# Weight sums of seven block products: from VectorE additions to accumulating transfers on GpSimd's queue, with tiles moved by 32 bytes

## The chip, the cores and the metric

The kernel runs on one core of one Trainium2 chip, in one launch. The metric is the time of one execution in microseconds (us); the time before is a median of 449.09 us over 3 runs (448.83 to 450.26). The weights stand in the chip's main memory (HBM) and are brought into SBUF, the on-chip memory that the engines read. Each engine works through its instructions in order: PE (TensorE, matrix products), ACT (ScalarE), DVE (VectorE), POOL (GpSimd) and SP (SyncE, which only issues transfers here). A transfer can be issued by SP or by POOL; the engine that issues it goes on, and the sixteen DMA engines of the core carry it out.

## The reference

One layer on 256 tokens of width 1024, everything in f32:

```
h = rms_norm(x, mix_norm_gain)
proj = h @ w_in                      # 1024 x 6144
xa, ga, qm, km, vm, qx, g_logits = split(proj)
y_a = rg_lru(conv(xa)) * gelu(ga)    # recurrent branch, width 512
y_b = block attention(qm, km, vm)    # width 512
y_c = cross attention(qx, mem)       # width 512
gates = sigmoid(g_logits).reshape(256, 3, 1024)
merged = sum over n of gates[n] * (y_n @ w_branch[n])
x = x + merged @ w_out
h = rms_norm(x, ffn_norm_gain)
x = x + (gelu(conv(h @ w_ffn_gate)) * (h @ w_ffn_up)) @ w_ffn_down
return rms_norm(x, final_norm_gain)
```

The change touches one piece of `proj`: the 1024 columns of `g_logits` that belong to gate 0 (`h` with a 1024 x 1024 part of `w_in`).

## The kernel before

**Weights as units.** All weight matrices are packed ahead of the launch into one array `ws` of units of 128 x 2048 f32 (1 MB). A unit is loaded by SP into a tile `wraw` (three buffers, L143). ACT rounds it to the high part `whi` (L189), and DVE subtracts that from the unit to get the low part `wlo` (L190); in the text, this pair is called the split of a unit. TensorE then makes each product as three matmuls: high x high, high x low, low x high. `ahead()` runs after each unit is consumed: it issues loads up to 4 steps ahead and splits up to 2 steps ahead. Two sequences made by `unit_plan()` set this: `PLAN` (which unit is which piece of a weight) and `STEPS` (in which order units are split and used). A scheduler of the framework then places each instruction on its engine's list by the order in which the program writes it and by what each needs; tiles come from pools with a fixed number of buffers, so a load or a split also waits until its buffer is free.

**Gate 0 by seven products.** The weight of gate 0 is cut into 2 x 2 blocks of one unit each, B11, B12 (the second 512 columns), B21 and B22 (the second half of the contraction). The 256 tokens are cut into two halves, so that the activations too form 2 x 2 blocks. Gate 0 needs seven block products (`product()`, L779) in place of eight: with B11, B21 and B22 themselves, and with four sums, T1 = B11 + B12, T3 = B12 + B22, T2 = T1 + B22 and T4 = T2 + B21. The activations' sums S1 to S4 are in the tiles `sh` and `sl`. The products stand between other units in the order of `STEPS`: B11, branch(1,0), T2, branch(2,0), T1, a half of gate(1,1), T3, its other half, B21, branch(1,1), B22, a half of gate(2,1), T4. `branch(n, half)` multiplies the output of branch n with half of its projection; its matmuls are at L247 to L249, those of `product()` at L785.

**How the sums are made before.** `block_t1()` runs when B11 has been split: SP loads B12 as two tiles of 128 x 1024 (`b12`, L160), and two DVE additions (`add2()`, L155) add it to B11's own tile `wraw`, which becomes T1. `block_t2()` runs when T2 is to be split: SP loads B22 into `b22` (L166), two additions make T3 in place of B12, and two write T2 into two tiles `t2`. When T4 is due, two additions add B21 to `t2`. Each sum is then split like a unit, in two halves of 128 x 1024.

**What the names in the profile are.** The program's names lose their digits there: `b12` and `b22` read `b`, the tiles `t2` read `t`, `p1` reads `p`, `u2` reads `u`. `ybh`, `ych` and `ycl` are the high and low parts of the outputs of branch 1 and 2, `mg` the sum of the gated branches, `gt` a gate, `fgb` the broadcast final gain, which POOL loads by a transfer of its own much later (L904). `PAD` is the width of an unused tile at the start of the first pool; every tile of the pools behind it lies that much further in each partition of SBUF.

Of the kernel before, what the change touches and what calls it, by code (L numbers as in the profile page):

```python
# [11 lines left out]
OP = mybir.AluOpType  # L12
# [84 lines left out]


LAG = 2
PAD = 232  # L100
WARM = 8
PLAN, STEPS = unit_plan()
NU = len(PLAN) - 2
# [4 lines left out]
def hybrid_trunk(ctx: ExitStack, tc: tile.TileContext, ws, xw, xv, xn, mt, mn, pp, lw, fg, out):  # L108
    nc = tc.nc
    V, A, T, G = nc.vector, nc.scalar, nc.tensor, nc.gpsimd  # L110

    cst = ctx.enter_context(tc.tile_pool(name="cst", bufs=1))
    cst.tile([128, PAD], F32, name="pad")
    wp = ctx.enter_context(tc.tile_pool(name="wp", bufs=3))
# [19 lines left out]
    raw, hi, lo = {}, {}, {}  # L134
# [12 lines left out]
    blk = {}  # L147
    HW = UW // 2

    def halves(t):  # L150
        return [t[:, :HW], t[:, HW:]]

    def add2(o, a, b):
        for x, y, z in zip(o, a, b):
            V.tensor_add(x, y, z)  # L155

    def block_t1(b11):
        blk["B12"] = [s4("b12", sh=(128, HW)) for _ in range(2)]
        for t, c in zip(blk["B12"], (0, HW)):
            nc.sync.dma_start(t, ws[NU - 2, :, c:c + HW])  # L160
        blk["T1"] = halves(raw[b11])
        add2(blk["T1"], blk["T1"], blk["B12"])

    def block_t2():
        b22 = ip.tile([128, UW], F32, name="b22", tag="sc", bufs=1)
        nc.sync.dma_start(b22, ws[NU - 1])  # L166
        blk["B22"] = halves(b22)
        blk["T3"] = blk["B12"]
        add2(blk["T3"], blk["B12"], blk["B22"])
        blk["T2"] = [s4("t2", sh=(128, HW)) for _ in range(2)]  # L170
        add2(blk["T2"], blk["T1"], blk["B22"])

    def split_next(parts=1):
        i = st["spl"]
        u = STEPS[i]
        h = wp.tile([128, UW], F32R, name="whi")
        l = wp.tile([128, UW], F32R, name="wlo")
        if u == "T2":
            block_t2()
        elif u == "T4":  # L180
            blk["T4"] = blk["T2"]
            add2(blk["T4"], blk["T2"], halves(raw[i0["B21"]]))
        if isinstance(u, str):
            src = list(zip(blk[u], halves(h), halves(l)))
        else:
            w = UW // parts
            src = [[t[:, p * w:(p + 1) * w] for t in (raw[u], h, l)] for p in range(parts)]
        for r, hh, ll in src:
            A.copy(hh, r)  # L189
            V.tensor_sub(ll, r, hh.bitcast(F32))  # L190
        hi[i], lo[i] = h, l
        if u == i0["B11"]:
            block_t1(u)
        st["spl"] += 1

    T2S = STEPS.index("T2")
    i0 = {"B11": STEPS[T2S - 2], "B21": STEPS[STEPS.index("B22") - 2]}
# [7 lines left out]
    def ahead():  # L205
        u = st["u"] - 1
        n = max(x for x in STEPS[:min(u + LA_D, NS - 1) + 1] if not isinstance(x, str))
        while st["dma"] <= n:
            dma_next()
        while st["spl"] <= min(u + LA_S, NS - 1):  # L210
            split_next()
# [75 lines left out]
    for k in range(KC):  # L287
        t = ip.tile([128, 1024], F32, name="xw", tag="s4", bufs=15)
# [24 lines left out]
    def s4(nm, dt=F32, sh=(128, 4, S)):  # L313
        t = ip.tile(list(sh), dt, name=nm, tag="s4", bufs=15)
        return t
# [17 lines left out]
    for k in range(KC):  # L333
# [14 lines left out]
        for j, (a, b) in enumerate(((h, xh), (h, xl), (l, xh))):  # L348
            for m in range(4):
                c = slice(512 * (k % 4) + m * 128, 512 * (k % 4) + m * 128 + 128)  # L350
                T.matmul(b0[m][:, :S], lhsT=a[:, c], rhs=b[:, k, :], start=(k == 0 and j == 0),  # L351
                         stop=(k == KC - 1 and j == 2))
    st["spl"] = st["u"] = 2
    split_next(2)
    split_next(2)
    ahead()
    sq = s4("sq", sh=(128, D))
# [47 lines left out]
    e, z, y, q, n8 = [cst.tile([128, 4], F32, name=f"sp{i}") for i in range(5)]  # L405
# [308 lines left out]
    sh, sl = a8p.tile([128, 4, 4, 128], F32R, name="sh", tag="a8"), a8p.tile([128, 4, 4, 128], F32R, name="sl", tag="a8")  # L714
# [135 lines left out]
    for i in range(2):  # L850
        t = a8p.tile([128, 4, 2, S], F32R, name="h2", tag="a8")
# [73 lines left out]
    def ffn_gate(f, bk):  # L925
        g = gp[f % 3]
        t = fp.tile([128, 2, S], F32, name="tcv", bufs=3)
        t2 = join(bk)
        V.tensor_mul(g[:, :, 2:], t2, rb2x)
        for m in range(2):  # L930
            b = 2 * f + m
            A.activation(t[:, m, :], g[:, m, 2:], AF.Identity, scale=par("fw", 48 + b), bias=par("fb", b))
            V.scalar_tensor_tensor(t[:, m, :], g[:, m, 1:1 + S], par("fw", 24 + b), t[:, m, :], op0=OP.mult, op1=OP.add)
            V.scalar_tensor_tensor(t[:, m, :], g[:, m, 0:S], par("fw", b), t[:, m, :], op0=OP.mult, op1=OP.add)  # L934
        A.activation(t, t, AF.Gelu_apprx_tanh)  # L935
        return t
# [45 lines left out]
    for f in range(1, 13):  # L982
        if f < 12:
# [4 lines left out]
            t = ffn_gate(f, gbk)  # L988
# [14 lines left out]
    for i, (t, c0, c1) in enumerate(FIN):  # L1003
        o = dz[i - 3][:, :256] if i > 2 else db[t][c0 // 512][:, c0 % 512:c0 % 512 + c1 - c0]
        V.scalar_tensor_tensor(yf[:, t, c0:c1], o, rs2[:, t:t + 1], (yf if i > 2 else x2)[:, t, c0:c1], op0=OP.mult,
                               op1=OP.add)
        x = slice(t, t + 1)
# [98 lines left out]
```

## Time and profile before

| | before |
|---|---|
| median of 3 runs | 449.09 us (448.83 to 450.26) |
| profiled execution, whole | 449.81 us |
| its span, first to last instruction | 448.0 us |
| mean granted TensorE clock | 0.994 of full speed |
| PE busy | 438.4 us, 98% of the span |
| DVE busy | 345.5 us, 77% |
| ACT busy | 274.9 us, 61% |
| POOL busy | 18.9 us, 4% |
| moved by transfers | 84.38 MB, mean 188 GB/s |

The span is shorter than the execution by what lies around it, 1.8 us here, and the profiled execution is 0.72 us above the median of the runs. Busy shares are means over the whole span. To find where an engine that is busy 98% of the time still loses some, one looks at shares in short stretches, at the waits of that engine, and then at the list of instructions around a wait. The granted clock is given as a share of 2.4 GHz: 1.00 is that level, 0.50 is 1.2 GHz.

### The profile page before, as it was taken

The numbers are of one execution on the slowest core, as the hardware profiler recorded it, in microseconds if no ns is written. First come the engines' busy times: TensorE is split into PE (matmuls) and PEld (weight loads), VectorE is DVE, ScalarE is ACT, GpSimd is POOL, SyncE is SP. The second block draws the span as 40 slices with busy tenths as digits, with TensorE's granted clock in tenths as the row PEclk, the third lists the DMA queues.
The fourth block names the chain that finished last, engine by engine and source line by source line (L and its number), as shares of the span: only waits on it lengthen the run. The fifth ranks groups of instructions, "written<-read, shape, count | busy, mean of one in ns | idle before, by whom it ended". The sixth has DMA issues, their size and how long they took to land.

```text
span 448.0 us, 6270 instructions
## 1 busy us (share of the span) xinstructions
PE 438.4 (98%) x2486; PEld 383.2 (86%) x2486; DVE 345.5 (77%) x458; ACT 274.9 (61%) x374; POOL 18.9 (4%) x21
## 2 busy tenths in 40 slices
PE   9999999999999899999999999999999999999994
PEld 9999879998888688888888888888888888888883
DVE  6679799999699997848767798766676677677664
ACT  6675989986655547554347676554554554554543
POOL 2000200130000000000001200000000000000011
PEclk9999999999999899999999999999999999999999
DMA  8975753556525356265445555545545555545102
GB/s 300 412 283 189 282 197 140 189 191 223 191 93 189 98 192 274 94 228 201 168 169 199 199 203 189 189 181 190 195 178 200 196 178 208 193 162 222 53 0 94
DMA packets 13852, 84.38 MB, mean 188 GB/s; under 512 B 1792, under 2 KB 2304, under 8 KB 4608
## 3 DMA queue, kind: packets, MB, share of 16 engines
q1 hardware_dynamic: 13392, 82.95, 50.3%
q0 software_dynamic: 144, 0.52, 0.5%
q10 hardware_dynamic: 288, 0.52, 0.3%
q8 instruction: 19, 0.31, 0.3%
q14 instruction: 9, 0.07, 0.0%
HBM read 82.94 MB, written 1.05 MB: 187 GB/s over the span
## 4 chain that ended last, share of the span: by engine, by line
PE 91%; DVE 6%; ACT 1%; issue 1%; DVEq 0%; ACTq 0%
PE mm L234 18%; PE mm L237 9%; PE ac L976 5%; PE ac L977 5%; PE ac L978 5%; PE ac L247 4%; PE ac L248 4%; PE ac L249 4%; PE mm L785 4%; PE mm L247 3%; PE mm L248 3%; PE mm L249 3%; PE mm L219 3%; PE mm L220 3%; PE mm L221 3%; PE mm L351 3%
## 5 line engine op out<-in xcount | busy, mean ns | idle before, releaser
L190 DVE TENSOR_TENSOR wlo<-wraw,whi 128x2048 fp32r<-128x2048 f32 (+1 forms) x74 | 164.1, 2220 | 68.8 <-ACT whi L189 68.5
L189 ACT CAST whi<-wraw 128x2048 fp32r<-128x2048 f32 (+1 forms) x74 | 135.9, 1839 | 79.4 <-PE mm L234 29.8
L234 PE MATMUL mm<-h,whi 128*128 128x512 f32 x352 | 88.8, 392 | 0.0
L234 PEld LDWEIGHTS mm<-h,whi 128*128 128x128 f32 x352 | 63.7, 189 | 11.6
L237 PEld LDWEIGHTS mm<-h,wlo 128*128 128x128 f32 x352 | 48.6, 190 | 3.8
L237 PE MATMUL mm<-h,wlo 128*128 128x256 f32 x352 | 49.7, 282 | 0.0
L976 PE MATMUL ac<-whi,ah 128*128 128x512 f32 x92 | 35.9, 392 | 0.0
L977 PE MATMUL ac<-wlo,ah 128*128 128x512 f32 x92 | 35.8, 391 | 0.0
L978 PE MATMUL ac<-whi,al 128*128 128x512 f32 x92 | 35.7, 390 | 0.0
L921 ACT COPY join<-mm 128x256 f32<-128x256 f32 x44 | 15.9, 364 | 18.6 <-PE mm L237 18.5
L935 ACT ACTIVATE tcv<-tcv 128x512 f32<-128x512 f32 x12 | 7.6, 632 | 27.0 <-DVE tcv L934 27.0
L219 PE MATMUL mm<-xh,whi 128*128 128x256 f32 x80 | 22.8, 284 | 0.0
L220 PE MATMUL mm<-xl,whi 128*128 128x256 f32 x80 | 22.6, 283 | 0.0
L221 PE MATMUL mm<-xh,wlo 128*128 128x256 f32 x80 | 22.6, 283 | 0.0
L978 PEld LDWEIGHTS ac<-whi,al 128*128 128x128 f32 x92 | 17.3, 188 | 3.8 <-DVE al L945 0.2
L976 PEld LDWEIGHTS ac<-whi,ah 128*128 128x128 f32 x92 | 17.3, 188 | 3.5 <-ACT ah L944 0.3
L977 PEld LDWEIGHTS ac<-wlo,ah 128*128 128x128 f32 x92 | 17.3, 188 | 3.2
L247 PE MATMUL mm<-whi,xh 128*128 128x512 f32 x48 | 18.9, 395 | 0.0
L249 PE MATMUL mm<-whi,xl 128*128 128x512 f32 x48 | 18.8, 392 | 0.0
L248 PE MATMUL mm<-wlo,xh 128*128 128x512 f32 x48 | 18.7, 391 | 0.0
L922 DVE TENSOR_TENSOR join<-mm,join 128x256 f32<-128x256 f32 x44 | 17.4, 417 | 0.3 <-ACT join L921 0.3
L219 PEld LDWEIGHTS mm<-xh,whi 128*128 128x128 f32 x80 | 15.4, 192 | 0.3 <-issue 0.3
(332 smaller groups left out, 914.5 us busy)
## 6 DMA issues: line engine op xcount, KB each, us to landing
wraw<-in_ws_dram SPq DMA_DIRECT2D x68, 1024.0 KB, 4.8
xw<-in_xv_dram SPq DMA_DIRECT2D x6, 388.0 KB, 6.4
wraw<-in_ws_dram SPq DMA_DIRECT2D x4, 512.0 KB, 9.9
x<-in_xn_dram SPq DMA_DIRECT2D x1, 1024.0 KB, 13.8
mnat<-in_mn_dram SPq DMA_DIRECT2D x1, 1024.0 KB, 5.5
mr<-in_mt_dram SPq DMA_DIRECT2D x1, 1024.0 KB, 4.8
b<-in_ws_dram SPq DMA_DIRECT2D x2, 512.0 KB, 6.8
b<-in_ws_dram SPq DMA_DIRECT2D x1, 1024.0 KB, 4.7
```

The lines of the kernel that those rows point to most:

```text
L189: A.copy(hh, r)
L190: V.tensor_sub(ll, r, hh.bitcast(F32))
L219: T.matmul(banks[m], lhsT=wh[:, k, c], rhs=rh[:, k, :], start=(k == 0), stop=False)
L220: T.matmul(banks[m], lhsT=wh[:, k, c], rhs=rl[:, k, :], start=False, stop=False)
L234: T.matmul(banks[m], lhsT=wh[:, k, c], rhs=hc[k // 4][:, k % 4].rearrange("p a t -> p (a t)"), start=(k == 0), stop=False)
L237: T.matmul(banks[m][:, :S], lhsT=wl[:, k, c], rhs=hc[k // 4][:, k % 4, 0, :], start=False, stop=(k == KC - 1))
L247: T.matmul(banks[t], lhsT=ah[:, k0 + k, s], rhs=wh[:, k, :], start=first and k == 0, stop=False)
L248: T.matmul(banks[t], lhsT=ah[:, k0 + k, s], rhs=wl[:, k, :], start=False, stop=False)
L249: T.matmul(banks[t], lhsT=al[:, k0 + k, s], rhs=wh[:, k, :], start=False, stop=last and k == 3)
L976: T.matmul(o, lhsT=ah[:, k, s], rhs=wh[:, k, cs], start=first, stop=False)
L977: T.matmul(o, lhsT=ah[:, k, s], rhs=wl[:, k, cs], start=False, stop=False)
L978: T.matmul(o, lhsT=al[:, k, s], rhs=wh[:, k, cs], start=False, stop=end)
```

## The change

`add2()` goes. A new helper `to(o, u, op)` issues two transfers on POOL, one for each half of unit `u` (128 x 1024, 0.52 MB each), from `ws` into the two tiles of `o`. With `accum_op` add, the transfer adds to what stands in the tile; without, it overwrites. T1 is made by adding B12 from HBM into B11's tile, T3 by adding B22 into `b12`, T4 by adding B21 into `t2`. T2 no longer starts from T1: its two tiles are allocated at `block_t1()`, get a plain load of B11 and then B12 and B22 added by transfer. In all that is 12 transfers of 0.52 MB on POOL (2 plain, 10 accumulating), and 8 DVE additions less. SP loads B12 and B22 into `b12` and `b22` as before; B22's tile is still split for its own product. `PAD` goes from 232 to 224 f32 words: all tiles behind it lie 32 bytes lower, and those of the weight pools start on multiples of 1024 bytes.

```diff
--- before.py
+++ after.py
@@ -97,7 +97,7 @@
 
 
 LAG = 2
-PAD = 232
+PAD = 224
 WARM = 8
 PLAN, STEPS = unit_plan()
 NU = len(PLAN) - 2
@@ -150,25 +150,27 @@
     def halves(t):
         return [t[:, :HW], t[:, HW:]]
 
-    def add2(o, a, b):
-        for x, y, z in zip(o, a, b):
-            V.tensor_add(x, y, z)
+    def to(o, u, op=OP.bypass):
+        for t, c in zip(o, (0, HW)):
+            G.dma_start(t, ws[u, :, c:c + HW], accum_op=op)
 
     def block_t1(b11):
         blk["B12"] = [s4("b12", sh=(128, HW)) for _ in range(2)]
         for t, c in zip(blk["B12"], (0, HW)):
             nc.sync.dma_start(t, ws[NU - 2, :, c:c + HW])
         blk["T1"] = halves(raw[b11])
-        add2(blk["T1"], blk["T1"], blk["B12"])
+        to(blk["T1"], NU - 2, OP.add)
+        blk["T2"] = [s4("t2", sh=(128, HW)) for _ in range(2)]
+        to(blk["T2"], b11 - 2)
+        to(blk["T2"], NU - 2, OP.add)
+        to(blk["T2"], NU - 1, OP.add)
 
     def block_t2():
         b22 = ip.tile([128, UW], F32, name="b22", tag="sc", bufs=1)
         nc.sync.dma_start(b22, ws[NU - 1])
         blk["B22"] = halves(b22)
         blk["T3"] = blk["B12"]
-        add2(blk["T3"], blk["B12"], blk["B22"])
-        blk["T2"] = [s4("t2", sh=(128, HW)) for _ in range(2)]
-        add2(blk["T2"], blk["T1"], blk["B22"])
+        to(blk["T3"], NU - 1, OP.add)
 
     def split_next(parts=1):
         i = st["spl"]
@@ -179,7 +181,7 @@
             block_t2()
         elif u == "T4":
             blk["T4"] = blk["T2"]
-            add2(blk["T4"], blk["T2"], halves(raw[i0["B21"]]))
+            to(blk["T4"], i0["B21"] - 2, OP.add)
         if isinstance(u, str):
             src = list(zip(blk[u], halves(h), halves(l)))
         else:
```

In the lists below a row gives line, operation, tiles and shape; the numbers behind names tell tiles of one name apart.

On POOL, the rows between its last arithmetic in the middle part and the load of `fgb`; before:

```order
L620 TENSOR_TENSOR ga_t_834<-ga_t_834,th_832 128x1024
L904 DMA fgb_2380<-in_fg_dram 128x1024
```

And of the kernel after the change:

```order
L622 TENSOR_TENSOR ga_t_834<-ga_t_834,th_832 128x1024
L155 DMA t2_1478<-in_ws_dram 128x1024
L155 DMA t2_1479<-in_ws_dram 128x1024
L155 DMA wraw_1347<-in_ws_dram 128x1024 x2
L155 DMA t2_1478<-in_ws_dram 128x1024
L155 DMA t2_1479<-in_ws_dram 128x1024
L155 DMA b12_1472<-in_ws_dram 128x1024
L155 DMA t2_1478<-in_ws_dram 128x1024
L155 DMA t2_1479<-in_ws_dram 128x1024
L155 DMA b12_1473<-in_ws_dram 128x1024
L155 DMA t2_1478<-in_ws_dram 128x1024
L155 DMA t2_1479<-in_ws_dram 128x1024
```

Twelve transfers have come into POOL's list: the two plain loads of T2's tiles, T1's two, T2's with B12, the first of T3, T2's with B22, the second of T3, and T4's two. T2 is whole after the ninth.

On ACT, the rows around the split of T2, with the unit of branch(2,0) (the first 128x2048) and T1 (the two 128x1024 of `wraw`) behind it; before:

```order
L736 ACTIVATE gt<-mm,rs_293 128x512
L683 CAST ych<-ac 128x256
L802 COPY p_1633<-mm 128x512
L189 CAST whi<-t_1625 128x1024
L189 CAST whi<-wraw 128x2048
L189 CAST whi<-t_1626 128x1024
L189 CAST whi<-wraw 128x1024 x2
```

And of the kernel after the change:

```order
L738 ACTIVATE gt<-mm,rs_293 128x512 x2
L685 CAST ych<-ac 128x256 x2
L191 CAST whi<-t_1478 128x1024
L191 CAST whi<-t_1479 128x1024
L804 COPY p_1637<-mm 128x512
L191 CAST whi<-wraw 128x2048
L191 CAST whi<-wraw 128x1024 x2
```

Both halves of T2 now stand ahead of the copy of `p` and of the unit of branch(2,0).

On SP, the loads after B12; before:

```order
L160 DMA b12_1473<-in_ws_dram 128x1024
L166 DMA b22_1621<-in_ws_dram 128x2048
L143 DMA wraw_1664<-in_ws_dram 128x2048
```

And of the kernel after the change:

```order
L160 DMA b12_1473<-in_ws_dram 128x1024
L143 DMA wraw_1668<-in_ws_dram 128x2048
L170 DMA b22_1629<-in_ws_dram 128x2048
```

The next unit of `wraw` has gone ahead of B22.

## Rows read from the trace of the kernel before

**Rows 1.** Page: busy us (share of the span) x instructions, of each engine.

```profile
PE 438.4 (98%) x2486; PEld 383.2 (86%) x2486; DVE 345.5 (77%) x458; ACT 274.9 (61%) x374; POOL 18.9 (4%) x21
```

**Rows 2.** Waits of PE, 100 to 220: us in total, times, longest.

```profile
PE ac L247 <- ACT whi L189: 1.3, 1, 1.3
PE mm L785 <- DVE t L155: 0.9, 1, 0.9
```

**Rows 3.** PE in order of time: start, duration, instruction, idle before and releaser.

```profile
141.88 0.28 PE L435 MATMUL ac<-pl,mvh 128*128 128x256 f32 x1
...
142.48 0.40 PE L247 MATMUL ac<-whi,ybh 128*128 128x512 f32 x1
...
146.36 0.39 PE L249 MATMUL ac<-whi,ybl 128*128 128x512 f32 x1
147.61 0.50 PE L785 MATMUL mm<-whi,sh 128*128 128x512 f32 x1 [0.87 <-DVE t L155]
149.42 0.80 PE L247 MATMUL ac<-whi,ych 128*128 128x512 f32 x1 [1.30 <-ACT whi L189]
150.01 0.63 PE L785 MATMUL mm<-wlo,sh 128*128 128x512 f32 x1
...
153.15 0.39 PE L248 MATMUL ac<-wlo,ych 128*128 128x512 f32 x1
```

**Rows 4.** Windows: us; busy of PE, PEld, DVE, ACT, POOL; PEclk, DMA share, GB/s.

```profile
138.00:140.00 2.00, 2.00 (x11) 1.65 (x10) 2.00 (x5) 1.94 (x3) 0.00 (x0) 1.00 1.05 442
141.00:146.00 5.00, 5.00 (x26) 4.24 (x25) 5.00 (x7) 2.58 (x5) 0.00 (x0) 1.00 0.01 3
150.00:151.00 1.00, 1.00 (x4) 0.80 (x3) 1.00 (x1) 1.00 (x2) 0.00 (x0) 0.50 0.00 0
250.00:448.00 198.00, 191.59 (x1023) 165.23 (x1021) 141.30 (x188) 109.99 (x143) 4.16 (x3) 1.00 0.46 166
```

**Rows 5.** DVE in order of time.

```profile
124.33 2.28 DVE L190 TENSOR_TENSOR wlo<-wraw,whi 128x2048 fp32r<-128x2048 f32 x1
...
141.47 1.22 DVE L155 TENSOR_TENSOR b<-b,b 128x1024 f32<-128x1024 f32 x1
...
145.20 2.36 DVE L155 TENSOR_TENSOR t<-wraw,b 128x1024 f32<-128x1024 f32 x2
...
166.28 2.35 DVE L155 TENSOR_TENSOR t<-t,wraw 128x1024 f32<-128x1024 f32 x2
```

**Rows 6.** ACT in order of time.

```profile
142.98 0.61 ACT L802 COPY p<-mm 128x512 f32<-128x512 f32 x1
146.52 1.04 ACT L189 CAST whi<-t 128x1024 fp32r<-128x1024 f32 x1 [2.93 <-DVE t L155]
147.47 1.90 ACT L189 CAST whi<-wraw 128x2048 fp32r<-128x2048 f32 x1
...
159.47 2.01 ACT L189 CAST whi<-b 128x1024 fp32r<-128x1024 f32 x2 [1.71 <-PE ac L249]
```

**Rows 7.** SP's issues in order of time.

```profile
134.15 0.33 SPq L166 DMA_DIRECT2D b<-in_ws_dram  x1
136.48 73.64 SPq L143 DMA_DIRECT2D wraw<-in_ws_dram  x13
```

**Rows 8.** POOL's one transfer, in order of time.

```profile
243.95 0.74 POOL L904 DMA_DIRECT2D fgb<-in_fg_dram  x1 [144.06 <-ACT sq L865]
```

**Rows 9.** DMA issues: engine, operation, KB each, median us from issue to landing.

```profile
fgb<-in_fg_dram POOLq DMA_DIRECT2D x1, 512.0 KB, 4.7
```

**Rows 10.** DMA queues: packets, MB, share of 16 engines' span (q0 is POOL's).

```profile
q1 hardware_dynamic: 13392, 82.95, 50.3%
q0 software_dynamic: 144, 0.52, 0.5%
```

**Rows 11.** DVE by line and form: count; busy us, mean ns.

```profile
L934 DVE SCALAR_TENSOR_TENSOR tcv<-gp,ppb,tcv 128x256 f32<-128x256 f32 x24 | 10.5, 479 | 0.0
L933 DVE SCALAR_TENSOR_TENSOR tcv<-gp,ppb,tcv 128x256 f32<-128x256 f32 x24 | 10.5, 479 | 0.0
```

## The prediction

> **What bounds the kernel now.** I read the page first: PE is busy for 438.4 of 448.0 us [rows 1], so a change moves the end only through what PE loses or stops losing. A stretch such as 250 to 448 shows 191.59 busy of 198 us at full clock [rows 4]: there is no slack in which a late PE could catch up, so a stall of PE in the middle is paid in full at the end. Next, the waits of PE in the stretch that the change touches: there are two, 0.9 us on the DVE addition that makes T2 and 1.3 us on the ACT cast of the unit of branch(2,0), which stands behind T2's cast [rows 2]. Last, PE's list around them. Matmuls follow each other every 0.228 us up to 146.36 (17 intervals from 142.48, 3.88 us). From there to 153.15 there are eleven intervals, 6.79 us, where 2.51 would do [rows 3]. The loss is 4.28 us: 2.17 in the two waits, 2.11 in matmuls at half the pace, since the granted clock fell to 0.50, 1.2 GHz, after them [rows 4].
>
> Why T2 is late: DVE is busy without a break from 141 to 146 [rows 4], and T2's additions come at the end of its queue, at 145.20; ACT had been idle for 2.93 us before it could cast the first half [rows 5, 6].
>
> **The most that the change can win.** It takes eight additions off DVE: T3's two of 1.22 and three pairs of about 2.36, 9.5 us [rows 5]. On DVE they are worth nothing by themselves; what they are worth is the 4.28 us, if T2 is in place in time. Then the profiled execution of 449.81 would be 445.5. The median of the runs lies 0.72 below that execution, so I take 0.72 off at the end: 444.8.
>
> **When T2 is ready.** Nine POOL transfers lead up to it. The two plain loads are done well before. The other seven go out behind one wait: T1's transfer must not write over B11 before DVE has split it, at 124.33 + 2.28 = 126.6 [rows 5]. Everything behind it on POOL's list waits too; nothing else of POOL's does, since its next work is at 243.95 [rows 8]. The only POOL transfer before took 4.7 us from issue to landing [rows 9], of which its engine time is 0.5% of 448 = 2.2 us [rows 10]; so 2.5 us are latency, paid once, since the next transfers of the list cover it for each dependent one. SP's next unit and B22, 2.1 MB, fall into the same stretch: they went out at 134.15 and 136.48 [rows 7] and still do within a few us. At 442 GB/s they take 4.74 us, with a share of 1.05 of all DMA engines [rows 4], so nothing is left beside them. With s for the engine time of one accumulating transfer of 0.52 MB, T2 is whole at 126.6 + 2.5 + 4.75 + 7s = 133.85 + 7s.
>
> The Trainium skill says the same of sharing: in "DMA: Bandwidth & Descriptors", section "Issuing engines are not separate DMA queues", transfers of SP and GpSimd interleave on the same 16 engines. By it the 4.75 stays in the sum; if it fell away, s = 2.5 would give 7s − 14.75 = 2.75 us of stall and about no change. No row of before has both queues busy at once.
>
> **When T2 is needed.** ACT reaches T2's cast after the gates, where the copy of `p` stood: 142.98 [rows 6]. In ACT's new order the second half of T2, the copy and the unit of branch(2,0) follow. After T2's landing come a cast of 1.04, the copy of 0.61, the cast of 1.90 [rows 6] and DVE's subtraction of 2.28 [rows 5]: 5.83, and 5.7 with the overlap of successive instructions. PE wants the low part of that unit for the second matmul of branch(2,0). Without a stall that is after the last matmul of branch(1,0) (146.36 + 0.23), twelve of T2's product (2.74) and one more (0.23): 149.55. So T2 has until 143.85, and the stall is 133.85 + 7s − 143.85 = 7s − 10 us.
>
> **What s is.** No row shows an accumulating transfer. Bounds from rows: SP's queue moves 82.95 MB in 50.3% of 448 us [rows 10], or 1.42 us for 0.52 MB, which I take as the lower end; POOL's plain transfer took 2.2. If the transfer reads both the tile and HBM, and reading is what takes the time, these double: 2.84 and 4.4, the upper end. The row of the same queue and the same size is the nearest, 2.2; since an accumulating transfer has to fetch more than a plain one, I go half way from it to 2.84 and take 2.5.
>
> On this the Trainium skill speaks against the change: "Collectives: The Full Stack", section "The bandwidth ceiling: the fold count and why AG ≠ RS ≠ AR", says that an adding transfer is slower not by its addition but by its two source reads, which halve its rate. With that, on the rate of the hardware queue, s is 2.84 and the sum below would come to 456.8. No row of before tests it.
>
> **The sum.** At s = 2.5 the stall is 7.5 us. The wait of 2.17 us cost 2.11 more by the clock, so I add 2.1. Against it stand the 4.28 that go: 7.5 + 2.1 − 4.28 = +5.3. The profiled execution would be 455.1, the median 454.4. At the ends: 1.42 gives a stall of nothing and 444.8; 4.4 gives 20.8 + 2.1 − 4.28 = +18.6 and 467.7. Break-even is at 7s − 10 + 2.1 = 4.28, s = 1.74.
>
> **The edits that I put at nothing.** T1 is in place at about 126.6 + 2.5 + 2 × 2.5 = 134, long before its cast behind T2. The second half of T3 lands one transfer behind T2, at 153.9 for s = 2.5, against a cast at 159.47 that moves later by the stall [rows 6]. T4's two transfers wait for T2's split; 7.5 us after that is some 162, against an addition at 166.28 before [rows 5]. POOL's issuing, 0.74 us each [rows 8], 5.2 for the seven, is hidden by their 7s. B22 now leaves behind the `wraw` unit, but no POOL transfer reads it (they read HBM), and its own split comes after branch(1,1). The extra 6.3 MB at SP's pace are 6.3 / 82.95 of 50.3%, about 4% of the engines' span, where they have half free; only the stretch counted above is crowded. That the tiles lie 32 bytes lower I put at nothing: DVE reads operands that begin 4 bytes apart in the same 479 ns [rows 11]. What the matmul does with it no row shows. Its interval is 0.120 us for 256 columns (five from 141.88 to 142.48) and 0.228 for 512 [rows 3], so 0.012 of each does not grow with the columns; 2486 times that [rows 1], 30 us, bounds what alignment could take away or add there. I see no ground for any of it, take 0, and leave it to the chances.
>
> **Rivals.**
> First, T2 in time: if an accumulating transfer costs what SP's plain ones do, s = 1.42 and 7s = 9.9, or if POOL's transfers and SP's slip through each other so that the 4.75 us vanish and s is below 2.1, T2 is whole by 143.85 and all of the loss goes: 444.8. For it speak the DMA engines' 0.01 share from 141 to 146 [rows 4], that is, time enough after SP's burst; against it, that the one transfer of POOL's queue was slower than SP's.
> Second, an even result: s between 1.55 and 2.0, a stall of 0.9 to 4 us in place of the old one; 448 to 451. That is also the case in which the change does not do what it says, with the wait on T2 put down to POOL's transfer instead of DVE.
> Third, dear accumulation: s above 3.2, 12.4 us of stall or more, 459.3 up to 467.7. The doubled price of POOL's own row speaks for it; the idle DMA engines after 141, which let the transfers run at their best, against.
> Fourth, the new alignment itself gives more than 1 us. Nothing in the rows speaks for it.
>
> **How the numbers follow.** The forecast, s from 2.0 to 3.2 (450.9 to 459.3), has 0.45; T2 in time 0.30; the even result 0.10; dear accumulation 0.13; alignment 0.02. A measurement of this kernel tells about 0.3%, 1.35 us, from no change. Faster: 0.30 + 0.02 = 0.32. Same: 0.10. Slower: 0.45 + 0.13 = 0.58. The range runs from 444.5, with the whole rival of T2 in time, to 462.0, which is s = 3.6; less than 2 in 10 lie outside. For the forecast alone it is 450.9 to 459.3.
>
> **What would show it.** Right: PE waits on ACT or DVE for `t2` some 7 us in one piece around 147 to 157, ACT's cast of `t2` starts when a POOL transfer lands, at about 151, and seven POOL transfers take some 17 us of engine time with SP's two between them; the last stretch keeps its pace. Wrong: T2's cast starts by 143 and PE has no gap there (the first rival); transfers from issue to landing of under 5 us in the middle of the chain; the interval of PE's matmuls differs from 0.228 us (the alignment); or a gap of PE before T3's or T4's product instead.

## The result and the profile after

| | before | after |
|---|---|---|
| median of the runs on one chip | 448.96 us (448.78 to 450.26, 4 runs) | 456.84 us (456.47 to 457.17, 4 runs) |
| profiled execution, its span | 449.81, 448.0 us | 456.47, 454.3 us |
| mean granted clock | 0.994 | 0.984 |

The change makes the kernel slower by 7.9 us: the ratio of the means is 1.0169, with a 95% interval from 1.0148 to 1.0190. Forecast were 454.4 and a range from 444.5 to 462.0. One run of those told of below is left out of its numbers, a run of 1546.68 us of the kernel before with `PAD` at 224.

PE's waits over the whole run after the change (us in total, times, longest), against [rows 2]:

```profile
PE mm L787 <- ACT whi L191: 5.8, 1, 5.8
...
PE mm L787 <- DVE wlo L192: 0.5, 1, 0.5
PE ac L250 <- DVE wlo L192: 0.4, 1, 0.4
```

And PE's list around them (start, duration, instruction, idle before and releaser), against [rows 3]:

```profile
146.75 0.39 PE L251 MATMUL ac<-whi,ybl 128*128 128x512 f32 x1
152.93 0.80 PE L787 MATMUL mm<-whi,sh 128*128 128x512 f32 x1 [5.80 <-ACT whi L191]
154.19 0.79 PE L787 MATMUL mm<-wlo,sh 128*128 128x512 f32 x1 [0.46 <-DVE wlo L192]
154.78 0.63 PE L787 MATMUL mm<-whi,sl 128*128 128x512 f32 x1
...
159.05 0.63 PE L249 MATMUL ac<-whi,ych 128*128 128x512 f32 x1
160.09 0.50 PE L250 MATMUL ac<-wlo,ych 128*128 128x512 f32 x1 [0.41 <-DVE wlo L192]
160.42 0.40 PE L251 MATMUL ac<-whi,ycl 128*128 128x512 f32 x1
160.66 0.39 PE L249 MATMUL ac<-whi,ych 128*128 128x512 f32 x1
```

The gap is in the place where it was, between branch(1,0) and T2's product, and it has grown. From 146.75 to 160.66 there are 16 intervals, 13.91 us, where 16 × 0.228 = 3.65 would do: 10.26 us are lost, against 4.28 before. That is 6.0 of the 6.3 us by which the span grew. Another 0.4 had come before it: branch(1,0)'s last matmul starts at 146.75 against 146.36 [rows 3]. What follows is 0.1 shorter.

Why PE waits stands in ACT's list, against [rows 6]; the columns are the same:

```profile
141.44 0.65 ACT L685 CAST ych<-ac 128x256 fp32r<-128x256 f32 x2
151.83 1.04 ACT L191 CAST whi<-t 128x1024 fp32r<-128x1024 f32 x1 [9.75 <-DMA t<-in_ws_dram]
154.38 1.04 ACT L191 CAST whi<-t 128x1024 fp32r<-128x1024 f32 x1 [1.50 <-DMA t<-in_ws_dram]
155.33 0.58 ACT L804 COPY p<-mm 128x512 f32<-128x512 f32 x1
155.81 5.61 ACT L191 CAST whi<-wraw 128x2048 fp32r<-128x2048 f32 x4
```

ACT is done with its earlier work at 142.1 and then stands for 9.75 us until the first half of T2 lands, and for another 1.50 until the second does; before, it waited 2.93 us for a DVE addition. DVE, which had no break from 141 to 146 before [rows 4], now waits 10.31 us behind ACT at the same place: the additions have gone, and nothing uses the room.

Two rows of DVE, the split of B11 and the low part of T2's first half:

```profile
124.45 2.28 DVE L192 TENSOR_TENSOR wlo<-wraw,whi 128x2048 fp32r<-128x2048 f32 x1
...
152.91 1.22 DVE L192 TENSOR_TENSOR wlo<-t,whi 128x1024 fp32r<-128x1024 f32 x1 [10.31 <-ACT whi L191]
```

POOL's list, which before held nothing between 99.9 and 243.95 [rows 8]:

```profile
109.30 0.54 POOL L155 DMA_DIRECT2D t<-in_ws_dram  x1 [0.48 <-PE ac L586]
127.04 1.82 POOL L155 DMA_DIRECT2D wraw<-in_ws_dram  x2 [17.21 <-DVE rsx L663]
128.17 2.48 POOL L155 DMA_DIRECT2D t<-in_ws_dram  x2
129.25 2.30 POOL L155 DMA_DIRECT2D b<-in_ws_dram  x1
139.33 0.87 POOL L155 DMA_DIRECT2D t<-in_ws_dram  x1 [7.79 <-DMA t<-in_ws_dram]
145.53 0.86 POOL L155 DMA_DIRECT2D t<-in_ws_dram  x1 [5.33 <-DMA t<-in_ws_dram]
```

T2's plain loads go out by 109.30, and then the queue stands still for 17.21 us, until DVE has split B11, at 124.45 + 2.28 = 126.73; the profile names `rsx`, which is DVE's next instruction behind that split. Only then T1's transfers, T2's with B12, T3's first and T2's with B22 follow.

The rate of these transfers is read in windows (us; busy of PE, PEld, DVE, ACT, POOL; PEclk, DMA share, GB/s):

```profile
137.00:141.00 4.00, 4.00 (x25) 3.54 (x24) 3.56 (x6) 3.97 (x7) 0.87 (x1) 1.00 1.03 320
141.00:145.00 4.00, 4.00 (x20) 3.30 (x19) 0.75 (x2) 1.08 (x3) 0.00 (x0) 1.00 1.04 312
149.00:154.00 5.00, 0.80 (x1) 0.29 (x1) 1.09 (x1) 1.04 (x1) 0.00 (x0) 0.56 1.06 211
154.00:160.00 6.00, 5.49 (x12) 3.64 (x12) 4.22 (x5) 5.62 (x6) 1.74 (x2) 0.51 0.84 143
```

From 149 to 154 only POOL's transfers move. All DMA engines are busy (1.06), and they bring 211 GB/s, where SP's plain loads brought 442 at the same share [rows 4]: 0.524 MB take 2.48 us. From 137 to 145 both queues share the engines, at a rate between the two.

### The profile page after: what moved, and what is told of

The parts are those of the page before. It is cut to its first block, busy times and chain, and to the rows that moved or that the text cites. A ratio compares the mean times of both kernels' runs of the same rounds, so it can differ in the third digit from the quotient of the medians.

```text
span 454.3 us, 6302 instructions
## 1 busy us (share of the span) xinstructions
PE 440.2 (97%) x2486; PEld 383.5 (84%) x2486; DVE 337.0 (74%) x450; ACT 274.7 (60%) x374; POOL 28.8 (6%) x33
## 3 DMA queue, kind: packets, MB, share of 16 engines
HBM read 89.24 MB, written 1.05 MB: 199 GB/s over the span
## 4 chain that ended last, share of the span: by engine, by line
PE 89%; DMA 6%; DVE 2%; ACT 1%; issue 0%; POOL 0%; DVEq 0%; ACTq 0%
PE mm L236 18%; PE mm L239 9%; DMA t<-in_ws_dram 6%; PE ac L978 5%; PE ac L979 5%; PE ac L980 5%; PE ac L250 4%; PE ac L251 4%; PE ac L249 4%; PE mm L249 3%; PE mm L250 3%; PE mm L251 3%; PE mm L221 3%; PE mm L787 3%; PE mm L222 3%; PE mm L223 3%
```

## The experiments

The runs of the kernel before that were taken with the first four kernels have a median of 450.16 us (448.84 to 450.73, 17 runs), those with the last four 449.58 (448.31 to 450.40, 17 runs). Ratios are against these.

**T2's transfers first.** `to()` now returns the last transfer it issued, and `tc.issue_after` puts T1's and T3's transfers behind T2's on POOL's list; no other engine's list changes.

```diff
...
         to(blk["T2"], b11 - 2)
         to(blk["T2"], NU - 2, OP.add)
-        to(blk["T2"], NU - 1, OP.add)
+        with tc.issue_after(to(blk["T2"], NU - 1, OP.add)):
+            blk["q"] = to(blk["T1"], NU - 2, OP.add)
...
-        to(blk["T3"], NU - 1, OP.add)
+        with tc.issue_after(blk["q"]):
+            to(blk["T3"], NU - 1, OP.add)
```

> The changed kernel with one thing moved: on GpSimd's list the four transfers that add B12 and B22 to T2's tiles stand ahead of T1's and T3's, so they no longer wait for the split of B11 and start as soon as T2's plain loads have landed, near 112 us. All other engines keep their lists. Theory (T2 comes late because seven transfers of 2.5 us stand in one queue behind the wait at 127 us): T2 is whole by some 125 us, ACT casts it at 142, PE has no gap between branch(1,0) and T2's product, and the 10.3 us that PE lost there go: about 446.5 us. Rival (ACT's new order, both halves of T2 ahead of the copy and of branch(2,0)'s unit, makes the gap): no change, about 456.8. Rival (the extra 6.3 MB slow the loads wherever they are put): between the two, with PE waiting for a unit of wraw.

Measured: 446.53 us (446.29 to 446.64), ratio 0.9922 (0.9909 to 0.9935). POOL's list and ACT's in this kernel:

```profile
113.27 0.90 POOL L155 DMA_DIRECT2D t<-in_ws_dram  x1 [3.06 <-DMA t<-in_ws_dram]
116.17 0.89 POOL L155 DMA_DIRECT2D t<-in_ws_dram  x1 [2.00 <-DMA t<-in_ws_dram]
122.68 0.86 POOL L155 DMA_DIRECT2D t<-in_ws_dram  x1 [5.62 <-DMA t<-in_ws_dram]
126.43 0.86 POOL L155 DMA_DIRECT2D t<-in_ws_dram  x1 [2.88 <-DMA t<-in_ws_dram]
127.41 1.76 POOL L155 DMA_DIRECT2D wraw<-in_ws_dram  x2
```

```profile
142.33 2.02 ACT L193 CAST whi<-t 128x1024 fp32r<-128x1024 f32 x2
144.24 0.61 ACT L806 COPY p<-mm 128x512 f32<-128x512 f32 x1
144.71 1.95 ACT L193 CAST whi<-wraw 128x2048 fp32r<-128x2048 f32 x1
```

All four accumulations of T2 are issued before T1's, and ACT casts both halves at 142.33 without a wait, in the order in which they stood after the change. PE has no wait in this part. So neither ACT's order nor the extra 6.3 MB made the gap; T2's place in the queue did.

**The alignment alone, at both kernels.**

```diff
-PAD = 224
+PAD = 232
```

> The changed kernel with the first tile back at 232 words, so that all tiles lie 32 bytes higher, as before the change, and nothing else. Theory (the alignment does nothing): 456.8, within 0.3%. Rival (operands on multiples of 1024 bytes cost or give something): the time moves by more than 1.4 us either way, and the interval of PE's matmuls or the mean of a DVE subtraction of 2048 columns differs from 0.228 us and 2.31 us.

Measured: 456.83 us (456.41 to 457.51), ratio 1.0155 (1.0139 to 1.0172), as the changed kernel.

> The kernel before with the first tile at 224 words, so that all tiles lie 32 bytes lower, and nothing else: the alignment alone. Theory: 449.0, within 0.3%. Rival: moved by more than 1.4 us, in the same direction as the difference between the changed kernel and its variant with 232 words.

Measured: 449.68 us (448.39 to 450.49, 11 runs), ratio 0.9992 (0.9980 to 1.0003). DVE's subtraction of 2048 columns takes 2309 ns in both kernels, and 2308 in those they come from; PE's matmuls of 512 columns still start 0.227 to 0.229 us apart. The 32 bytes do nothing that can be measured.

**The same transfers, plain.** They overwrite their tiles, so no weight sum is made.

```diff
-            G.dma_start(t, ws[u, :, c:c + HW], accum_op=op)
+            G.dma_start(t, ws[u, :, c:c + HW], accum_op=OP.bypass)
```

> The changed kernel with its ten accumulating transfers made plain: same tiles, sizes, waits and order, but each overwrites its tile, so that no weight sum is made. Theory (an accumulating transfer reads its tile as well as HBM and takes about twice the engine time of a plain one, 2.5 us against 1.3): the seven transfers take about 8 us less, T2 lands near 146.5 instead of 154.4, PE loses some 2.3 us instead of 10.3, and the time is about 449. Rival (GpSimd's queue is slow for any transfer): 456.8, T2 still near 154.

Measured: 448.31 us (448.00 to 448.45), ratio 0.9961 (0.9946 to 0.9976). T2's halves are cast at 143.30 and 146.37, and PE waits 1.7 us, for the split of branch(2,0)'s unit:

```profile
143.30 1.05 ACT L191 CAST whi<-t 128x1024 fp32r<-128x1024 f32 x1 [0.87 <-DMA t<-in_ws_dram]
146.37 1.05 ACT L191 CAST whi<-t 128x1024 fp32r<-128x1024 f32 x1 [2.02 <-DMA t<-in_ws_dram]
```

The share of POOL's queue (packets, MB, share of 16 engines' span), here and after the change, in this order:

```profile
q0 software_dynamic: 1872, 6.82, 4.4%
```

```profile
q0 software_dynamic: 1872, 6.82, 7.1%
```

That is 19.6 us of engine time here and 32.3 after the change, for thirteen transfers of the same size of which ten differ: 1.27 us more for each. A plain one took 19.6 / 13 = 1.51, so an accumulating one 2.78, 1.84 times as much (both with waits for the other queue in them). Packet by packet it is about double: one of 4 KB in POOL's queue takes 159 ns here and 328 after the change (medians).

**B22's own load later.** SP's 1 MB load of B22 goes behind the next `wraw` unit; only SP's list changes.

```diff
-        nc.sync.dma_start(b22, ws[NU - 1])
+        blk["b22"], blk["n"] = b22, len(raw)
...
+        if "b22" in blk and len(raw) == blk["n"] + 1:
+            with tc.issue_after(d.ins):
+                nc.sync.dma_start(blk["b22"], ws[NU - 1])
```

> The changed kernel with SP's load of B22 (1 MB, needed for B22's own product only) put behind the next wraw unit, so that it leaves at about 160 instead of 135.7 us; all other lists stay. Theory (the transfers of SP and GpSimd share the same DMA engines, and T2 waits for the sum of both): 1.05 MB at 442 GB/s, 2.4 us, go out of the stretch, T2 lands near 152.0 instead of 154.4, and the time falls to about 454.4. Rival (the landing of dependent transfers sets the pace of the chain, whatever SP moves): 456.8.

Measured: 454.37 us (454.06 to 454.62), ratio 1.0104 (1.0089 to 1.0119), 2.5 below the changed kernel (2.3 to 2.9 by the ratios, since the two were not taken together). ACT's list here:

```profile
150.06 1.04 ACT L195 CAST whi<-t 128x1024 fp32r<-128x1024 f32 x1 [7.56 <-DMA t<-in_ws_dram]
152.55 1.04 ACT L195 CAST whi<-t 128x1024 fp32r<-128x1024 f32 x1 [1.44 <-DMA t<-in_ws_dram]
```

T1's transfers were issued 0.42 later in this execution (127.46), T2 lands 1.83 earlier: the chain is 2.25 us shorter. 1.05 MB at 442 GB/s are 2.37 us, so the chain paid for these bytes of the other queue about the price that they have alone.

**Early T2 on DVE.** From the kernel before: no transfer on POOL; B22 is also loaded into T2's tiles, by SP, and added there.

```diff
         add2(blk["T1"], blk["T1"], blk["B12"])
+        blk["T2"] = [s4("t2", sh=(128, HW)) for _ in range(2)]
+        for t, c in zip(blk["T2"], (0, HW)):
+            nc.sync.dma_start(t, ws[NU - 1, :, c:c + HW])
+        add2(blk["T2"], blk["T1"], blk["T2"])
...
-        add2(blk["T3"], blk["B12"], blk["B22"])
-        blk["T2"] = [s4("t2", sh=(128, HW)) for _ in range(2)]
-        add2(blk["T2"], blk["T1"], blk["B22"])
...
+        elif u == "T3":
+            add2(blk["T3"], blk["B12"], blk["B22"])
```

> The kernel before, with no transfer on GpSimd's queue for the sums: SP also loads B22 into T2's two tiles, which are free near 110 us, right behind B12; DVE adds T1 to them right behind T1's own additions, near 130, and T3's additions are written where T3 is split. DVE does the same eight additions. Theory (only the time at which T2 is ready matters, not which engine makes the sums): the 4.3 us that PE loses there go but for some tenths, about 446. Rival (DVE is too full between 125 and 150 for any order to help): 448.5 to 450, with PE waiting on DVE for T2 or for the unit of branch(2,0).

Measured: 447.94 us (447.39 to 449.89, 12 runs), ratio 0.9971 (0.9957 to 0.9986): 1.6 us won of some 4 expected. In the profiled execution (449.89) T2 is cast at 137.82, but PE now waits one step earlier:

```profile
141.75 0.39 PE L788 MATMUL mm<-whi,sh 128*128 128x512 f32 x1
143.93 0.50 PE L250 MATMUL ac<-whi,ybh 128*128 128x512 f32 x1 [1.79 <-DVE ycl L687]
```

This execution is the slowest of the twelve: behind the wait PE's matmuls ran at half the pace from 145.43 to 148.81 (granted clock 0.50), 1.6 us more, and the runs with a mean clock of 0.996 or more take 447.4 to 448.1. The subtractions `ycl` read the PSUM banks (TensorE's output buffers) that branch(1,0) writes next. They come late on DVE's list, behind the early additions, and DVE has no break from 122 to 144; on ACT, T2's casts now also stand ahead of the casts that `ycl` needs. Which of the two counts for more no run isolates. So the expectation held half: the time of T2 matters whoever makes it, but taking the work off DVE seems to be worth something too, since here an earlier T2 came with a later `ycl`.

**T2 and T4 on POOL, T1 and T3 on DVE.**

```diff
+    def add2(o, a, b):
+        for x, y, z in zip(o, a, b):
+            V.tensor_add(x, y, z)
...
-        to(blk["T1"], NU - 2, OP.add)
+        add2(blk["T1"], blk["T1"], blk["B12"])
...
-        to(blk["T3"], NU - 1, OP.add)
+        add2(blk["T3"], blk["B12"], blk["B22"])
```

> The changed kernel with T1 and T3 made by DVE additions again, T2 and T4 by GpSimd's transfers: six transfers less, and T2's chain no longer behind the wait at 127 us. Theory: as with T2's transfers put first, about 446.5, no gap of PE before T2's product. Rival (DVE's four additions push the split of branch(2,0)'s unit late): 448 or more, with PE waiting on DVE there.

Measured: 454.23 us (453.12 to 455.39), ratio 1.0105 (1.0086 to 1.0123). The theory's number missed; the time is in the rival's range, but not by its way. T2 was early (its last transfer went out at 125.46), and the wait is before it, in DVE's list and then PE's:

```profile
129.97 1.23 DVE L155 TENSOR_TENSOR wraw<-wraw,b 128x1024 f32<-128x1024 f32 x1 [1.56 <-DMA b<-in_ws_dram]
133.70 1.22 DVE L155 TENSOR_TENSOR wraw<-wraw,b 128x1024 f32<-128x1024 f32 x1 [2.50 <-DMA b<-in_ws_dram]
134.84 1.28 DVE L669 TENSOR_TENSOR px<-px,rsx 128x512 f32<-128x512 f32 x2
```

```profile
135.68 0.99 PE L677 MATMUL ac<-ident,px 128*128 128x128 f32 x4 [4.00 <-DVE px L669]
```

T2's transfers now run beside SP's loads of B12, which T1's additions need. Those loads took 11.5 us to land in this kernel (the last number of a row), 6.8 before the change and after it, and DVE stood behind them with `px`, for which PE waited 4.00 us. It waited another 1.40 for `ycl`, later on the same list. In the version with T2's transfers first the same loads took 12.8 us, but there nothing needs them early, since T1 takes B12 from HBM. The loads in this kernel, after the change, and with T2's transfers first:

```profile
b<-in_ws_dram SPq DMA_DIRECT2D x2, 512.0 KB, 11.5
```

```profile
b<-in_ws_dram SPq DMA_DIRECT2D x2, 512.0 KB, 6.8
```

```profile
b<-in_ws_dram SPq DMA_DIRECT2D x2, 512.0 KB, 12.8
```

**The best version once more.**

> The version with T2's transfers ahead of T1's and T3's once more, beside the two others: 446.5 again by all theories; it is there to tell which of the three is fastest on one chip.

Measured: 446.06 us (445.74 to 446.73), ratio 0.9922 (0.9909 to 0.9936). It is the fastest of all kernels here, 0.8% below the one before.

## Why the prediction was right

The mechanism came out as forecast: T2 whole too late in POOL's queue, ACT blocked in order, PE idle before T2's product, 5.80 us of it in one piece. That the number came as near as it did is in part luck: one term was too small and another too large. Its terms, one by one:

- **POOL's start.** Forecast 126.6, from DVE's split of B11; the transfers went out at 127.04.
- **s, the price of an accumulating transfer.** Forecast 2.5; 2.48 where they run alone. So close a hit is luck. The 2.5 lay half way between POOL's one row of 2.2 and 2.84, and the 2.2 is not what a plain transfer of weights costs there: the experiment has 1.51, so POOL's plain transfers are hardly dearer than SP's 1.42. What holds is the doubling, which the prediction took as an upper end: 2.48 is about twice the 0.524 MB / 442 GB/s = 1.19 of a plain transfer at the full rate. The Trainium skill's rule ("Collectives: The Full Stack", "The bandwidth ceiling: the fold count and why AG ≠ RS ≠ AR"), that an adding transfer reads two sources and so has half the rate, is stated there for a reduction between cores; the trace agrees with 211 against 442 GB/s at a full share. That the prediction's sum by this rule, 456.8, meets the measured time is chance too, since it holds the clock's 2.1 us (below).
- **The 4.74 us of SP's loads.** Half of it was tried, with B22's load moved out: 2.25 us instead of the 2.37 for half. The other half, the load of `wraw`, was not.
- **When T2 is whole.** Forecast 151.35; the second half was cast at 154.38, 3.0 late. 0.4 is the start. T1's two transfers ended at 135.0 (the mean of the sixteen engines, by the packets in the trace), where 126.6 + 2.5 + 5.0 = 134.1 was assumed, another 0.5. In the last transfer of T2 fifteen of the sixteen DMA engines were done at 152.8 and one at 154.0; the sum counted the mean engine, and the wait is for the last: 1.2. The rest, 0.9, lies between landing and cast (0.35) and in the shared stretch.
- **When it is needed.** The rule "T2 has until 143.85" held: 154.38 + 5.7 = 160.08 for the low part of branch(2,0)'s unit, and PE's matmul that needs it starts at 160.09. Without a wait it would have been due at 146.75 + 14 × 0.228 = 149.94, so the stall is 10.15, against 7.5 forecast: T2 was 3.0 later, but PE came to it 0.4 later too.
- **The clock.** This term failed: 2.1 us were added for matmuls at half the pace. They did run so (0.51 from 154 to 160), but under a wait that was longer: the last slow matmul, at 159.05, was over before the split of branch(2,0)'s unit came at 160.09. Loss and stall differ by 0.1 (10.26 and 10.15).
- **The sum.** 10.26 − 4.28 = 6.0 against 5.3 forecast: the stall 2.65 too small, the clock 2.0 too large, and the stall that goes as worked out. What lies around the span grew by 0.4 (456.47 − 454.3 against 449.81 − 448.0), which was not forecast. With this and the 0.3 that the rest of the span gained, the profiled execution is 6.7 longer; the medians are 7.9 apart, because the execution profiled before lay 0.85 above its median and the one after 0.37 below.
- **The edits put at nothing.** T1, T3 and T4 made no wait of PE. The alignment is 0 within the uncertainty of both runs.
- **The rivals.** T2 in time is out by s and the shared stretch, but its time was about right: with the queue in another order T2 is in time, the gap goes, and 0.9922 of 448.96 us is 445.5, against 444.8. An even result needed s below 2.0, dear accumulation s above 3.2. Between 137 and 145 the two queues together brought 312 to 320 GB/s at a share of 1.03 to 1.04, so what one moves the other waits for; with that the trace agrees with the Trainium skill ("DMA: Bandwidth & Descriptors", "Issuing engines are not separate DMA queues").

## What to carry to other kernels

An accumulating transfer takes an addition off an engine, but here it cost about twice a plain one on the DMA engines (328 against 159 ns for 4 KB), and it stands in its queue in order; add up all that the queue must do before the sum that is needed first, and put that sum's transfers first. When a sum on a busy engine is late, ask first what else stands ahead of it: the same change with one reordering was 10 us faster. Before moving transfers earlier, look at which loads they will then run beside, and who waits for those.

## What the runs showed of the hardware that was not expected

- The time around the span is 1.80 us for the kernel before (1.73 to 1.85, 17 runs), 1.78 for the variant with T2 early on DVE, which has none of the sums' transfers on POOL, 1.99 with eight more there than before, and 2.0 to 2.2 with twelve more (medians of a kernel's runs). What takes it was not tried.
- After the change, one DMA engine ended each of T2's last two transfers 1.2 us after the other fifteen (150.3 and 151.5, 152.8 and 154.0), although SP's transfers had ended at 148.4. Its packets took 328 ns as the others' did; it had fallen behind while both queues moved, by 0.4 us at 144.2 and 1.2 at 149.0, and why it did stays open.
- The same program's granted clock differs between executions: the runs of the kernel before with a mean clock of 0.997 or more take 448.3 to 449.6 us (both sets), those at 0.995 or less 449.7 to 450.7. The stretch after its gap at 1.2 GHz, which cost 2.1 us in the profiled execution at 0.994, is where such a difference can lie; no run isolates it.
- The mean clock alone does not tell the time: in the second set's profiled execution of the version with T2's transfers first, the record gives 0.95 in every stretch from 10 to 440 us (mean 0.946), yet its span is 444.4 us as in the first set at 0.997, and its matmuls of 512 columns still start 0.227 us apart.
